# Accumulating half-size products in PSUM chains, gate rows on ScalarE, and a four-bank recurrence in a two-layer Hawk/HGRN2 step

## The chip, the cores and the metric

The kernel runs on one core of a Trainium2 chip. A core has TensorE (PE: matmuls, with its weight loads counted apart as PEld), VectorE (DVE), ScalarE (ACT), GpSimd (POOL) and SyncE (SP), each with its own instruction stream that is executed in order. The engines meet through semaphores. Matmuls write PSUM, which this kernel uses as eight banks of 128 x 512 fp32. The metric is the device time of one execution in microseconds, lower is better; a comparison uses the median of several runs.

## What is computed

Two layers over 1056 tokens (1024 of a prompt and 8 x 4 of decoding sequences), model width 1024, all in fp32. The first is an RG-LRU block. The second, the one that this change touches, is an HGRN2 block with 8 heads of width 128:

```python
u = (xn @ w_in).astype(jnp.float32)
q, f, iv, gate = jnp.split(u, 4, axis=-1)
q = jax.nn.silu(q).reshape(Bsz, T, H_B, DK_B)
log_g = jnp.logaddexp(jnp.log(lbh), jnp.log1p(-lbh) + jax.nn.log_sigmoid(f...))
k = -jnp.expm1(log_g)
v = iv.reshape(Bsz, T, H_B, DV_B)
o, S_T = _hgrn2_chunked(q, k, v, log_g, S0)
o = o * lax.rsqrt(jnp.mean(o * o, axis=-1, keepdims=True) + EPS) * o_gain...
y = (o.reshape(Bsz, T, INNER_B) * jax.nn.silu(gate)).astype(x.dtype)
return x + y @ w_out, S_T.astype(x.dtype)
```

So each head needs four projections of 128 rows (q, f, v and the output gate), then a gated linear recurrence, then a norm over the head. The gate g is `lbc + lc * tanh(f/2)` and the key is `lc - lc * tanh(f/2)`: two rows that are affine in one tanh.

## The kernel before

**fp32 from three passes.** Every fp32 product is split: weight and activation are each a high and a low part, and `mm3` (L240) issues three matmuls, high x high, high x low, low x high, that add up in PSUM. ACT makes the high part of a weight (L1425, `whi<-wraw`), POOL the low part (L322, `wlo<-wraw,whi`).

**Layer 1 by heads.** Heads 0 and 1 are projected in the plain way (`item`, L993, and `product`, 352 columns at a time). Heads 2 to 7 are projected by `seven` (L1398), two calls for each head: one with order `FQ` for the rows q and f (items 0 and 1), then one with order `GV` for the output gate and v (items 3 and 2). A call treats a pair of rows as a 2 x 2 block product (two halves of the 1024 inputs, two halves of the tokens) and computes it by seven products of half size in place of eight: product 1 to product 7, each 128 x 512 weights against 528 tokens. Each is done in two quarters x = 0 and 1 of 264 tokens, 12 matmuls each, into a fresh bank `ps`. In this text "6x0" is quarter 0 of product 6. With P1 to P7 for the products, the results are

- row a, first half: P1 + P2
- row a, second half: P1 + P6 + P5 + P3
- row b, first half: P1 + P6 + P7 + P4
- row b, second half: P1 + P6 + P7 + P5

Before, ACT copies P1 out of its bank (L1468), and every further sum is an addition by DVE, `plus` (L1496), that reads one bank and one SBUF tile of 264 columns: 14 in a call. The three `mm` banks rotate, so a product's quarter may start when the quarter three places earlier has been read.

`settle` (L1498) ends a row: tanh on ACT, then for q and the output gate a multiply on DVE (L1511), and for f two rows by POOL (L1505: the gate `Gs`, L1506: the key `b`), 264 columns at a time. `item` does the same for head 1 in chunks of 352 (L1009, L1011).

**The recurrence in four bursts.** It is computed by doubling levels 1, 2, 4, ..., 64. Each level scales half of two rows by products of gates (`scale`, L1022: DVE L1033 and a gate product L1042, ACT copies the other half, L1036) and PE multiplies small diagonal blocks (`diag`, L1047). DVE keeps the blocks of each level in `ad` with masked copies (`keep`, L1055), and four DVE copies put them on the diagonal of the attention tile `at` (L1114). The PE work of the recurrence is grouped into bursts that stand between products: burst 1 (levels 0 and 1; transposes of keys and values of the head before), burst 2 (levels 2 and 4; the states of the head before, which DVE chains in `SA`, L1232 and L1234), burst 3 (outputs of the head before, levels 8 and 16), burst 4 (its gating, levels 32 and 64). The letters b in an order string are the bursts: `FQ` = "12b675b43" holds bursts 3 and 4, `GV` = "126b754b3" bursts 1 and 2. The first call, for head 2, has `FQ0` = "126b74b35". Each burst takes five or four of the five `hg` banks in turn, one of them (`s`) for small matmuls of the decoding sequences.

**What sets the order.** All work of layer 1 is recorded with estimated costs in a `Flow` (L51); a list scheduler fixes each engine's order from priorities and due times, and the instructions are then emitted in that order. PE's work is recorded as `main`, so its order is the one of the code. What the other engines do in between is decided by the planner.

Of the kernel before, what the change touches and what calls it, by code (L numbers as in the profile page):

```python
# [19 lines left out]
ALU = mybir.AluOpType  # L20
# [6 lines left out]
NMM = 3  # L27
HC = 2
NM7 = 3
FQ0, FQ, GV = "126b74b35", "12b675b43", "126b754b3"  # L30
# [180 lines left out]
def tile_trunk(ctx: ExitStack, tc: tile.TileContext, xT, prm, hc, w0, wg, wo0, w1, wo1, s_in,  # L211
# [28 lines left out]
    def mm3(out, w, xh, xl, first, last):  # L240
        wh, wl = w
        T.matmul(out, wh, xh, start=first, stop=False)  # L242
        T.matmul(out, wh, xl, start=False, stop=False)  # L243
        T.matmul(out, wl, xh, start=False, stop=last)  # L244
# [681 lines left out]
    with ExitStack() as l1:  # L926
# [3 lines left out]
        mm, hg = cycle(banks8[:NMM]), cycle(banks8[NMM:])  # L930
# [62 lines left out]
        def item(h, i):  # L993


            def evac(c, ps, pk):
# [10 lines left out]
                if i == 1:  # L1007
                    g, (b, bk) = Gs, brow(h, 1)
                    pool(CH, lambda: G.tensor_scalar(g[:, q], t, lc[:, h:h + 1], lbc[:, h:h + 1], op0=ALU.mult, op1=ALU.add),  # L1009
                         (tk,), GK, 0)  # L1010
                    pool(CH, lambda: G.tensor_scalar(b[:, q], t, lcn[:, h:h + 1], lc[:, h:h + 1], op0=ALU.mult, op1=ALU.add),  # L1011
                         (tk,), bk, 0)
# [85 lines left out]
        def levels816(h, p8, pk):  # L1098
# [13 lines left out]
            for j in range(4):  # L1112
                w = slice(32 * j, 32 * j + 32)
                dve(256, lambda w=w: V.tensor_copy(at[w, :, w], ad[w]), (("ad",),), (("at", 0),), 3)  # L1114
# [6 lines left out]
        def levels3264(h, ps, pk):  # L1121
# [17 lines left out]
            p64, qk = next(hg)  # L1139
            pe(0.56, emit64, (*ak, *bk), (qk,))  # L1140
# [3 lines left out]
            for i in range(2):  # L1144
# [3 lines left out]
                moved(i, 256, odd[:64, i, :, 64:], p64[64 * i:64 * i + 64, :256].rearrange("p (u t) -> p u t", u=4), qk, ("at", 2, i))  # L1148
# [156 lines left out]
        def gated(h, s, sk):  # L1305
# [10 lines left out]
            o = s[:, 256:288]  # L1316
# [10 lines left out]
        def burst1(h):  # L1327
            s = next(hg)
            run(together([*([levels01(h, *s)] if h < H else []), *([keys_(h - 1, *s), values(h - 1, (1,), *s)] if h else [])]))

        def burst2(h):
            s = next(hg)
# [65 lines left out]
        def seven(h, a, b, order, at=()):  # L1398
# [44 lines left out]
            late, mid, low = places  # L1443
            places = low, mid, late
            for c in order:
# [9 lines left out]
                for x in range(2):  # L1455
                    ps, pk = next(mm)
                    ops = [operand(p, j, x) for j in range(4)]

                    def emit(ps=ps, ops=ops, hi=hi, lo=lo):
# [7 lines left out]
                    if p == 1:  # L1467
                        act(QT, lambda o=late[x][0], z=z[0]: S.copy(o, z), (pk,), (late[x][1],), 0)  # L1468
                    elif p == 2:
                        plus(mid[x], z, late[x])  # L1470
                        ending(a, first, *mid[x])
                    elif p == 6:
                        plus(late[x], z, late[x])
                    elif p == 7:
                        plus(low[x], z, late[x])
                    elif p == 3:
                        plus(late[x], z, late[x])
                    else:
                        t, o = second if p == 5 else first, mid[x] if next(q for q in steps if q in (4, 5)) == p else low[x]
                        if b == 2:  # L1480
                            plus((VT[:, t:t + QT], ("VT", t // QT)), z, low[x])
                            if t + QT == TOK:
                                thrice(vrep, VT[:, SEQ:], (("VT", 3),), "vrep")
                        else:
                            plus(o, z, low[x])
                            ending(b, t, *o)
                        if p == 5:
                            plus(late[x], z, late[x])
                    if p == [q for q in steps if q in (3, 5)][1]:
                        ending(a, second, *late[x])  # L1490
# [317 lines left out]
```

## Time and profile before

| | |
|---|---|
| time, median of 3 runs | 1086.44 us (1086.31 to 1087.67) |
| span of the profiled execution (its own time is not given; the span is 2.2 us under the median) | 1084.3 us |
| PE busy | 97% of the span |
| DVE busy | 82% |
| POOL busy | 56% |
| ACT busy | 51% |
| granted TensorE clock, mean | 0.993 |

The span falls into layer 0 (up to about 520 us), heads 0 and 1 of layer 1 (about 520 to 600 us), heads 2 to 7 in `seven` (about 600 to 960 us), and the output projection with the final norm. A row of the timeline gives start, duration, engine, line, operation, tiles and shape, and in brackets how long the engine had been idle before it and on whom it waited. A PE matmul of 264 columns is shown with about 0.28 us, but one starts every 0.12 us, since they overlap; PE counts as idle only when none is in flight.

### The profile page before, as it was taken

How to read it: one execution, taken by the hardware profiler on the slowest of the kernel's cores; microseconds unless marked ns; L12 is line 12 of the kernel's file. 1: busy time of each engine (PE TensorE's matmuls, PEld its weight loads, DVE VectorE, ACT ScalarE, POOL GpSimd, SP SyncE). 2: the span in 40 equal slices, each digit the busy share in tenths (PEclk: the TensorE clock that was granted, in tenths of full speed). 3: DMA queues.
4: the chain of work that ended last, by engine and by line, in shares of the span. 5: the costliest groups of instructions: out<-in, count | busy, mean ns of one | idle time of the engine just before them, and what ended most of it. 6: DMA issues, size and time to landing. Idle time of an engine off the chain costs nothing.

```text
span 1084.3 us, 25492 instructions
## 1 busy us (share of the span) xinstructions
PE 1056.6 (97%) x9972; PEld 1027.9 (95%) x9972; DVE 885.3 (82%) x1661; ACT 549.2 (51%) x1249; POOL 602.3 (56%) x600
## 2 busy tenths in 40 slices
PE   9999999999999999999999999999999999999997
PEld 9999999999999999999899899999998989899996
DVE  8999995897996886275989999989989898995436
ACT  6578657868666964143433444443343434452323
POOL 3425453363452537356665876858686776752545
PEclk9999999999999999999999999999999999999998
DMA  9211222124822776240210121212121212355204
GB/s 299 60 26 42 56 55 66 55 67 133 279 83 66 223 251 180 95 134 30 60 41 24 48 92 43 99 44 89 39 77 51 89 42 67 111 179 164 77 7 160
DMA packets 70119, 103.05 MB, mean 95 GB/s; under 512 B 9200, under 2 KB 51184, under 8 KB 70000
## 3 DMA queue, kind: packets, MB, share of 16 engines
q1 hardware_dynamic: 67696, 98.67, 29.5%
q10 hardware_dynamic: 2304, 2.77, 0.7%
q8 instruction: 78, 1.28, 0.5%
q14 instruction: 41, 0.34, 0.1%
HBM read 71.05 MB, written 25.49 MB: 89 GB/s over the span
## 4 chain that ended last, share of the span: by engine, by line
PE 75%; DVE 20%; issue 3%; DMA 1%; POOL 0%; ACT 0%; POOLq 0%; ACTq 0%; DVEq 0%; SPq 0%
PE mm L242 21%; PE mm L243 20%; PE mm L244 20%; DVE k L1496 3%; DVE R L1033 2%; DVE sg L1042 2%; DVE sg L1033 2%; DVE R L1511 1%; PE hg L566 1%; DVE tmp L1365 1%; PE hg L1214 1%; PE hg L242 1%; PE hg L243 1%; PE hg L244 1%; PE hg L1268 1%
## 5 line engine op out<-in xcount | busy, mean ns | idle before, releaser
L242 PE MATMUL mm<-xh,whi 128*128 128x352 f32 (+1 forms) x1143 | 360.6, 315 | 1.7 <-DVE k L1496 1.6
L243 PE MATMUL mm<-xl,whi 128*128 128x352 f32 (+1 forms) x1143 | 354.4, 310 | 0.9 <-DVE xl L322 0.9
L244 PE MATMUL mm<-xh,wlo 128*128 128x352 f32 (+1 forms) x1143 | 354.2, 310 | 0.0
L322 POOL TENSOR_TENSOR wlo<-wraw,whi 128x512 fp32r<-128x512 f32 (+2 forms) x132 | 181.9, 1385 | 145.2 <-ACT whi L377 84.2
L242 PEld LDWEIGHTS mm<-xh,whi 128*128 128x128 f32 x1143 | 215.9, 189 | 4.4 <-DVE k L1496 2.5
L243 PEld LDWEIGHTS mm<-xl,whi 128*128 128x128 f32 x1143 | 216.2, 189 | 2.6 <-DVE xl L322 1.1
L244 PEld LDWEIGHTS mm<-xh,wlo 128*128 128x128 f32 x1143 | 216.0, 189 | 0.0
L498 DVE SCALAR_TENSOR_TENSOR k<-xb,prm_sb,k 128x352 f32<-128x352 f32 (+2 forms) x144 | 90.1, 637 | 10.9 <-ACT k L495 6.2
L242 PE MATMUL mm<-t,whi 128*128 128x264 f32 (+1 forms) x306 | 89.9, 294 | 7.1 <-DVE k L1496 7.1
L243 PE MATMUL mm<-t,whi 128*128 128x264 f32 (+1 forms) x306 | 87.7, 286 | 0.0
L244 PE MATMUL mm<-t,wlo 128*128 128x264 f32 (+1 forms) x306 | 87.6, 286 | 0.0
L581 POOL TENSOR_TENSOR k<-X 128x352 f32<-128x352 f32 x36 | 43.9, 1227 | 47.4 <-DVE R L582 37.8
L242 PEld LDWEIGHTS mm<-t,whi 128*128 128x128 f32 x306 | 57.6, 188 | 8.6 <-DVE k L1496 7.9
L1496 DVE TENSOR_TENSOR k<-mm,k 128x264 f32<-128x264 f32 x144 | 60.0, 425 | 5.2 <-issue 1.3
L322 POOL TENSOR_TENSOR wlo<-R,whi 128x512 fp32r<-128x512 f32 x32 | 46.1, 1442 | 28.1 <-ACT whi L1425 26.8
L377 ACT CAST whi<-wraw 128x512 fp32r<-128x512 f32 (+2 forms) x83 | 46.0, 574 | 29.9 <-PE mm L243 18.2
L244 PEld LDWEIGHTS mm<-t,wlo 128*128 128x128 f32 x306 | 57.6, 188 | 0.0
L243 PEld LDWEIGHTS mm<-t,whi 128*128 128x128 f32 x306 | 57.6, 188 | 0.0
L1033 DVE TENSOR_TENSOR R<-R,sg 128x512 f32<-128x512 f32 (+1 forms) x48 | 52.6, 1096 | 0.2
L242 PE MATMUL mm<-yh,whi 128*128 128x352 f32 x153 | 49.9, 326 | 0.0
L244 PE MATMUL mm<-yh,wlo 128*128 128x352 f32 x153 | 49.4, 323 | 0.0
L243 PE MATMUL mm<-yl,whi 128*128 128x352 f32 x153 | 49.4, 323 | 0.0
(479 smaller groups left out, 2714.8 us busy)
## 6 DMA issues: line engine op xcount, KB each, us to landing
wraw<-in_w_dram SPq DMA_DIRECT2D x90, 256.0 KB, 2.8
wraw<-in_wo_dram SPq DMA_DIRECT2D x34, 192.0 KB, 2.5
si<-in_s_in_dram SPq DMA_DIRECT2D x8, 512.0 KB, 4.6
out_ss_out_dram<-si SPq DMA_DIRECT2D x8, 512.0 KB, 2.6
R<-in_w_dram SPq DMA_DIRECT2D x15, 256.0 KB, 2.6
sg<-x1b SPq DMA_DIRECT2D x21, 176.0 KB, 2.9
x<-sg SPq DMA_DIRECT2D x21, 176.0 KB, 2.0
R<-td SPq DMA_DIRECT2D x72, 44.0 KB, 2.0
```

Source lines behind the costliest of these rows:

```text
L242: T.matmul(out, wh, xh, start=first, stop=False)
L243: T.matmul(out, wh, xl, start=False, stop=False)
L244: T.matmul(out, wl, xh, start=False, stop=last)
L322: emit = lambda: e.tensor_tensor(b, x, a.bitcast(F32), op=ALU.subtract)
L377: act(m, lambda hi=hi, raw=raw, m=m: S.copy(hi[:, :m], raw[:, :m]), rk, (hk,), prio)
L498: dve(u, lambda src=src, dst=dst, sh=sh, k=k: V.scalar_tensor_tensor(dst, sh(src, k), pc("cw", 12 * k + m), dst, op0=ALU.mult, op1=ALU.add ...
L566: fl.add("PE", 0.62, lambda ps=ps, i=i, c=c: T.matmul(ps[:96, :CH], gs[:, i, :], ST[:96, chunk(c)], start=True, stop=True), (("gs",), *((" ...
L581: pool(CH, lambda x=x, a=a, b=b: G.tensor_tensor(x, a.bitcast(F32), b.bitcast(F32), op=ALU.add), (ak, bk), (xk,), 3)
L1033: dve(n // 2, lambda sv=sv, dv=dv, s=s, f=f: V.tensor_tensor(dv[:, :, s, :], sv[:, :, s, :], f, op=ALU.mult), (*sk, *gk), dk if i == o els ...
L1042: dve(nb, lambda: V.tensor_tensor(g2, gv[:, :, 0], gv[:, :, 1], op=ALU.mult), gk, (k2,), 3, True)
L1214: T.matmul(ps[:, n * 128:(n + 1) * 128], kt[:, 4 * i + n, :], vt[:, 4 * i + n, :], start=True, stop=True)
L1496: dve(QT, lambda: V.tensor_tensor(o[0], z[0], u[0], op=ALU.add), (z[1], u[1]), (o[1],), 0)
```

## The change

**Chains.** `mm` in `seven` no longer rotates over three banks. Four banks are split into two chains of two, one bank for each quarter: `chains[0]` takes products 1, 6, 7, 4, and `chains[1]` takes 2, 5, 3. Products 6, 7 and 4 do not start a new sum: their first matmul adds to what stands in the bank. ACT copies P1, P1+P6 and P1+P6+P7 out of the bank (L1481 in the new file), and after product 4 the bank holds the whole sum of row b's first half, which `settle` reads directly (for v, ACT copies it to `VT`, L1488). Product 3 adds to product 5's bank where 5 comes first, and `plus` (now L1504) is left with P2, P5 and P3: 6 in a call, 8 in the `FQ0` call, where 3 comes before 5. ACT copies 6 in a call in place of 2, and 2 more in a `GV` call.

**Order.** `GV` becomes "126b74b53": one product fewer stands between bursts 1 and 2, one more after burst 2.

**Gate rows.** The two affine rows of f go from POOL to ACT (`Identity` with a scale and a bias for each partition; L1513, L1514, and in `item`).

**Diagonal copies.** The four copies into `at` for each head go from DVE to ACT (L1112).

**Banks.** `hg` has four banks; levels 32 and 64 share one bank; `s` of bursts 1 and 2 comes from `side`, which is the fourth bank outside `seven` and the two banks of `chains[1]` inside it.

```diff
-FQ0, FQ, GV = "126b74b35", "12b675b43", "126b754b3"
+FQ0, FQ, GV = "126b74b35", "12b675b43", "126b74b53"
...
-        mm, hg = cycle(banks8[:NMM]), cycle(banks8[NMM:])
+        mm, side, hg = cycle(banks8[:NMM]), cycle(banks8[NMM:4]), cycle(banks8[4:])
+        chains = banks8[:2], banks8[2:4]
...
             for j in range(4):
                 w = slice(32 * j, 32 * j + 32)
-                dve(256, lambda w=w: V.tensor_copy(at[w, :, w], ad[w]), (("ad",),), (("at", 0),), 3)
+                act(256, lambda w=w: S.copy(at[w, :, w], ad[w]), (("ad",),), (("at", 0),), 3)
...
-            p64, qk = next(hg)
-            pe(0.56, emit64, (*ak, *bk), (qk,))
+            p64 = ps[:, 128:384]
+            pe(0.56, emit64, (*ak, *bk), (pk,))
...
         def burst1(h):
-            s = next(hg)
+            s = next(side)
...
                 for x in range(2):
-                    ps, pk = next(mm)
+                    ps, pk = chains[p in (2, 3, 5)][x]
+                    new = p in (1, 2, 5) or apart and p == 3
...
-                            mm3(ps[:, :QT], (hi[:, w], lo[:, w]), uh, ul, j == 0, j == 3)
+                            mm3(ps[:, :QT], (hi[:, w], lo[:, w]), uh, ul, new and j == 0, j == 3, True)
...
+                    if p in (1, 6, 7):
+                        o = {1: one, 6: two_, 7: three}[p][x]
+                        act(QT, lambda o=o[0], z=z[0]: S.copy(o, z), (pk,), (o[1],), 0)
                     elif p == 2:
-                        plus(mid[x], z, late[x])
-                        ending(a, first, *mid[x])
-                    elif p == 6:
-                        plus(late[x], z, late[x])
-                    elif p == 7:
-                        plus(low[x], z, late[x])
-                    elif p == 3:
-                        plus(late[x], z, late[x])
+                        plus(one[x], z, one[x])
+                        done(a, first, *one[x])
+                    elif p == 4:
+                        if b == 2:
+                            o = home(b, first, None)
+                            act(QT, lambda o=o[0], z=z[0]: S.copy(o, z), (pk,), (o[1],), 0)
+                        done(b, first, *z)
                     else:
...
                         if p == 5:
-                            plus(late[x], z, late[x])
+                            o = home(b, second, three[x])
+                            plus(o, z, three[x])
+                            done(b, second, *o)
+                        if p == 3 or apart:
+                            plus(two_[x], z, two_[x])
...
-                pool(QT, lambda: G.tensor_scalar(Gs[:, q], b, lc[:, h:h + 1], lbc[:, h:h + 1], op0=ALU.mult, op1=ALU.add), bk, (g,), 0)
-                pool(QT, lambda: G.tensor_scalar(b, b, lcn[:, h:h + 1], lc[:, h:h + 1], op0=ALU.mult, op1=ALU.add), bk, bk, 0)
+                act(QT, lambda: S.activation(Gs[:, q], b, AF.Identity, bias=lbc[:, h:h + 1], scale=lc[:, h:h + 1]), bk, (g,), 0)
+                act(QT, lambda: S.activation(b, b, AF.Identity, bias=lc[:, h:h + 1], scale=lcn[:, h:h + 1]), bk, bk, 0)
...
-        mm, hg = cycle(banks8[:NM7]), cycle(banks8[NM7:])
+        side = cycle(banks8[NMM - 1:4])
```

The planner makes a new order from this. Three places of a head in the middle of the run (heads 3 to 7 read alike) matter for the prediction. In these rows `hg` and `mm` are banks, `attnd` is `ad`, `attns` its small version for the decoding sequences, `R`, `a` and `sg` are the rows that the levels scale, `k` the homes of partial sums. The new file's lines stand 1 to 8 higher or lower than the old ones: L1033 is L1031, L1055 is L1053, L1496 is L1504, L1036 is L1034.

DVE from the scalings after burst 1 to the one that burst 2 waits for, before:

```order
L1033 TENSOR_TENSOR R<-R,ST 128x528
L1033 TENSOR_TENSOR a<-a,ST 128x528
L1496 TENSOR_TENSOR k<-mm,k 128x264
L1058 COPY_PREDICATED attns<-mask_86,hg 32x32
L1058 COPY_PREDICATED attns<-mask_87,hg 32x32
L1496 TENSOR_TENSOR k<-mm,k 128x264
L1176 TENSOR_TENSOR kst<-hg,kst 32x128
L1176 TENSOR_TENSOR vst<-hg,vst 32x128
L1033 TENSOR_TENSOR R<-R,sg 128x264x2
L1496 TENSOR_TENSOR sg<-mm,k 128x264
L1496 TENSOR_TENSOR k<-mm,k 128x264
L1033 TENSOR_TENSOR sg<-a,sg 128x264x2
```

and in the change:

```order
L1031 TENSOR_TENSOR R<-R,ST 128x528
L1031 TENSOR_TENSOR a<-a,ST 128x528
L1031 TENSOR_TENSOR R<-R,sg 128x264x2
L1031 TENSOR_TENSOR sg<-a,sg 128x264x2
L1174 TENSOR_TENSOR vst<-mm,vst 32x128
L1174 TENSOR_TENSOR kst<-mm,kst 32x128
L1056 COPY_PREDICATED attns<-mask_86,mm 32x32
L1056 COPY_PREDICATED attns<-mask_87,mm 32x32
```

The four scalings of levels 1 and 2 now follow each other at once; the additions and the small copies between them are gone or stand behind.

DVE from burst 2 to the additions of product 5, which the banks of product 3 wait for, in the change (before, these additions were of products three places away):

```order
L1053 COPY_PREDICATED attnd<-mask_88,hg 128x256
L1053 COPY_PREDICATED attnd<-mask_89,hg 128x256
L1031 TENSOR_TENSOR sg<-sg 128x128x4
L1230 COPY a<-hg 128x128
L1232 SCALAR_TENSOR_TENSOR a<-a,gp,hg 128x128 x3
L1056 COPY_PREDICATED attns<-mask_88,mm 32x32
L1232 SCALAR_TENSOR_TENSOR a<-a,gp,hg 128x128 x4
L1248 SCALAR_TENSOR_TENSOR si<-si,gp,hg 128x128
L1031 TENSOR_TENSOR R<-R,sg 128x128x4
L1504 TENSOR_TENSOR sg<-mm,k 128x264 x2
```

The whole chain of states and the scaling of level 4 stand ahead of the two additions.

ACT in the same call, from burst 1 to the copies of 7x0 and 7x1 (the two rows L1481), in the change:

```order
L1164 COPY kt<-hg 128x512 x2
L1164 COPY sg<-hg 128x512
L1034 COPY R<-R 128x264x2
L1172 CAST vst<-mm 96x128
L1172 CAST kst<-mm 96x128
L1481 COPY k<-mm 128x264
L1034 COPY sg<-a 128x264x2
L1176 COPY vts<-mm 32x128
L1481 COPY k<-mm 128x264
```

Each copy out of a chain's bank stands behind a copy (L1034) that waits for DVE's scaling of level 1.

More of the change, by code (lines that the diff above doesn't have):

```diff
@@ L1442, in seven, with done, home @@
                 split(p)
-            late, mid, low = places
-            places = low, mid, late
+            one, two_, three = places
+            apart = steps.index(3) < steps.index(5)
+            def done(i, t, c, ck):
+                if i == 2:
+                    if t + QT == TOK:
+                        thrice(vrep, VT[:, SEQ:], (("VT", 3),), "vrep")
+                else:
+                    ending(i, t, c, ck)
+            def home(i, t, o):
+                return (VT[:, t:t + QT], ("VT", t // QT)) if i == 2 else o
             for c in order:
@@ L1598, in tile_trunk @@
         splits(5, range(NCH), G)
-        mm, hg = cycle(banks8[:NMM]), cycle(banks8[NMM:])
+        side = cycle(banks8[NMM:4])
         raws = cycle([r for r in rawq if r[1][0] == "raw"])
```

37 lines of the change are left out of this document (12 added, 25 removed).

## The prediction

> **What bounds the kernel now.** I read the page first, then the busy time by stretches, then who PE waits for, and last the timeline around those waits. The page's first and fourth parts:
>
> ```profile
> span 1084.3 us, 25492 instructions
> PE 1056.6 (97%) x9972; PEld 1027.9 (95%) x9972; DVE 885.3 (82%) x1661; ACT 549.2 (51%) x1249; POOL 602.3 (56%) x600
> ...
> PE 75%; DVE 20%; issue 3%; DMA 1%; POOL 0%; ACT 0%; POOLq 0%; ACTq 0%; DVEq 0%; SPq 0%
> ```
>
> PE is the bound: 1084.3 - 1056.6 leaves it idle for 27.7 us, and no change that keeps its matmuls can win more. This one keeps them all: 7 products x 2 quarters x 12 matmuls in each of 12 calls. But 20% of the chain that ended last is DVE. By stretches (columns: length, then busy time and instructions of each engine):
>
> ```profile
> core 0: us, PE busy (x) PEld busy (x) DVE busy (x) ACT busy (x) POOL busy (x), PEclk, DMA share, GB/s
> ...
> 749.30:808.60 59.30, 57.42 (x809) 55.19 (x808) 53.66 (x102) 24.36 (x67) 41.80 (x38) 1.00 0.21 65
> ```
>
> That is one head of the middle run: PE idle for 1.9 us, DVE busy for 53.7 of 59.3. The granted clock is 1.00, so PE's rate is not in question. Who PE waits for, in heads 0 to 2 (520 to 630 us of the span; columns: total, times, longest) and behind them (630 to 990):
>
> ```profile
> PE hg L1051 <- DVE sg L1033: 2.3, 1, 2.3
> PE hg L1105 <- DVE a L1033: 1.6, 1, 1.6
> PE hg L1160 <- DVE si L1250: 1.4, 1, 1.4
> PE mm L243 <- DVE xl L322: 0.9, 1, 0.9
> PE hg L1136 <- DVE sg L1033: 0.5, 1, 0.5
> ...
> PE mm L242 <- DVE k L1496: 8.7, 9, 1.5
> PE hg L1051 <- DVE sg L1033: 3.0, 4, 0.8
> ```
>
> Every wait is for DVE, 18.4 us in all. The rest of the 27.7 us lies in the start and in the final norm, which the change leaves. Two kinds recur in each head:
>
> ```profile
> 755.87 1.26 DVE L1063 TENSOR_TENSOR R<-R,ST 128x1056 f32<-128x1056 f32 x1
> 757.04 0.42 DVE L1496 TENSOR_TENSOR k<-mm,k 128x264 f32<-128x264 f32 x1
> ...
> 757.52 0.39 PE L242 MATMUL mm<-t,whi 128*128 128x264 f32 x1 [1.15 <-DVE k L1496]
> ...
> 759.18 1.10 PE L1051 MATMUL hg<-R,a 128*32 128x64 f32 x64
> ...
> 762.02 0.37 PE L242 MATMUL mm<-t,whi 128*128 128x264 f32 x1
> ...
> 762.59 0.93 DVE L1055 COPY_PREDICATED attnd<-mask,hg 128x256 f32<-128x256 uint8 x2
> ...
> 764.48 0.70 DVE L1033 TENSOR_TENSOR a<-a,ST 128x528 f32<-128x528 f32 x1
> ...
> 769.06 3.25 DVE L1033 TENSOR_TENSOR sg<-a,sg 128x528 f32<-128x528 f32 x1
> ...
> 771.82 1.63 POOL L1433 TENSOR_TENSOR R<-R,wraw 128x512 f32<-128x512 f32 x1
> ...
> 772.46 0.75 PE L1051 MATMUL hg<-R,sg 128*32 128x32 f32 x64 [0.73 <-DVE sg L1033]
> ```
>
> At 757.5 a product waits until its bank is read: the addition is short (0.42), but stood behind the 1.26 us of L1063. Burst 1 starts at 759.18, has its first blocks ready 1.1 us later and lasts 2.8 us; DVE comes to its masked copies at 762.59, 2.3 us late. At 772.5 the second half of burst 2 waits for a scaling that took 3.25 us where the same shape took 0.70 at 764.48, while POOL worked beside it. So DVE is late, partly by its own load, partly stretched by POOL.
>
> [...]
>
> **The change part by part.**
>
> ```profile
> L1496 DVE TENSOR_TENSOR k<-mm,k 128x264 f32<-128x264 f32 x144 | 60.0, 425 | 5.2 <-issue 1.3 <-PE mm L244 1.2
> L1114 DVE COPY attn<-attnd 32x256 f32<-32x256 f32 x32 | 17.3, 541 | 0.5
> L1505 POOL TENSOR_SCALAR ST<-a,smalls 128x264 f32<-128x264 f32 x24 | 15.4, 647 | 4.0 <-ACT a L1504 4.0
> L1506 POOL TENSOR_SCALAR a<-a,smalls 128x264 f32<-128x264 f32 x24 | 19.6, 825 | 0.2
> L1468 ACT COPY k<-mm 128x264 f32<-128x264 f32 x24 | 8.6, 374 | 6.5 <-PE mm L244 5.9
> L495 ACT ACTIVATE k<-xb,prm_sb 128x352 f32<-128x352 f32 x24 | 16.4, 681 | 3.2 <-DVE sg L528 1.8 <-DVE xb L479 0.9
> ```
>
> *DVE load.* A head loses 28 - 12 = 16 additions of 0.425 (6.8 us) and four diagonal copies of 0.541 (2.2 us): DVE falls from 53.7 to about 44.7 us of 59.3. POOL loses 4 x (0.647 + 0.825) = 5.9 of its 41.8 us.
>
> *ACT load.* A head gains 8 copies for the chains and 2 for v at 0.374 (3.7 us), 8 gate rows and 4 diagonal copies. The trace of before has no ACT instruction of 264 columns with a scale and a bias; the nearest, L495 with 352 columns, takes 0.681, and the plain copy of 264 takes 0.374, so a gate row lies between the two and I take 0.6, nearer to L495 since it is the same operation (8 x 0.6 = 4.8). A diagonal copy has 32 x 256 elements; I take 0.374 for it too (1.5). ACT rises from 24.4 to about 34.4 us of 59.3: room enough on average, and free where it does not queue.
>
> *What goes.* In `seven` I count the two recurring waits, 8.7 + 3.0 = 11.7 us, as gone, since DVE has 9 us less to do in each head and the additions that the first kind waited for (products 1, 6, 7 and 4) are now copies by an engine that is 58% busy. At the end of head 1, burst 4 waits 0.5 and 1.4 us for DVE, which ahead of it has additions of head 2's products 2, 6, 7 and 4 in its order (8 x 0.425 = 3.4 us); those of product 2 alone stay, 2.6 us go, so I count the 1.9 us as gone too. The waits of 2.3 and 1.6 us in heads 0 and 1 stay: DVE's order ahead of them is the same list of `build` additions, and no addition of `seven` lies there. The 0.9 us stays: product 5 of head 2 still waits for its operand, made by the same DVE and ACT steps. Gone: 11.7 + 1.9 = 13.6 us.
>
> *What comes.* A product that adds to its bank must wait until the bank has been read. Where a chain's products follow each other, only one quarter lies between, and the trace shows how long that is:
>
> ```profile
> 780.63 0.38 ACT L1468 COPY k<-mm 128x264 f32<-128x264 f32 x1
> ...
> 782.10 0.38 ACT L1468 COPY k<-mm 128x264 f32<-128x264 f32 x1 [1.09 <-PE mm L244]
> ```
>
> The two quarters of a product are 1.47 us apart, and the copy starts with the end of the product's last matmul, about 0.16 us behind the next one's first issue (0.28 against 0.12). The copy needs 0.38, so 1.47 - 0.16 - 0.38 leaves 0.9 us. Before, two quarters lay between, and 2.4 us were left. The places are 6 to 7 in `FQ` and 7 to 4 in `GV` (ACT), and 5 to 3 in `GV` (DVE).
>
> For the ACT places I add nothing. In `GV` 7x0's copy stands behind the ACT copy of level 1's scaled row; counted from burst 1's start, that scaling can end about 2.7 us in (blocks at 1.1, two masked copies 0.9, scaling 0.70), the ACT copy 0.7 us later, and 7x0 ends at 4.5 us. That ACT works off its queue in time is the cover; if it is gone, the cost is that of the last rival.
>
> For 5 to 3 the order rows give a wait. Burst 2 before, with the first product behind it:
>
> ```profile
> 770.95 0.73 PE L1051 MATMUL hg<-R,a 128*32 128x32 f32 x62
> ...
> 773.60 0.91 DVE L1055 COPY_PREDICATED attnd<-mask,hg 128x256 f32<-128x256 uint8 x2
> 774.40 0.98 DVE L1033 TENSOR_TENSOR sg<-sg 128x512 f32<-128x512 f32 x1
> ...
> 775.62 1.11 DVE L1234 SCALAR_TENSOR_TENSOR a<-a,gp,hg 128x128 f32<-128x128 f32 x3
> ...
> 776.04 0.29 PE L242 MATMUL mm<-xh,whi 128*128 128x264 f32 x1
> ...
> 778.70 0.68 DVE L1033 TENSOR_TENSOR R<-R,sg 128x512 f32<-128x512 f32 x1
> ```
>
> Without its 0.73 us wait the burst lasts 776.04 - 770.95 - 0.73 = 4.4 us, and 3x0 wants to start 2 x 1.47 later, at 7.3. DVE can start the masked copies when both levels are multiplied, at 1.5; they take 0.8, the scaling 0.9, the eight states 8 x 0.37 = 3.0, the small masked copy 0.1, one update of `si` (the size of a state) 0.4, the second scaling 0.7 to 1.1, and 5x0's addition 0.42. That is 7.7 to 8.1, and 3x0 waits 0.4 to 0.8 us. If DVE comes to burst 2 as late as before (773.60, 2.65 us in), it is 1.9; if the states overlap better, nothing. I take 0.8, since L1033 seldom runs at its shortest. Heads 3 to 7 have this order, so 5 x 0.8 = 4.0 us; in head 2 the additions stand earlier.
>
> **Sum.** -13.6 + 4.0 = -9.6 us: the span falls from 1084.3 to 1074.7, and the median, 2.1 us above it, from 1086.4 to 1076.8.
>
> **The rivals.** *All waits of `seven` go*, the one at product 3 too: 13.6 us, 1072.8. For it: DVE has 14 us of slack per head. Against: the order rows put all of burst 2's work on DVE ahead of the addition.
>
> *The wait at burst 2 grows.* With `GV`'s new order only products 7 and 4 lie between bursts 1 and 2, four quarters instead of six, 2.9 us less. Before, the last scaling (769.06 + 3.25) ended 13.1 us behind burst 1's start; the new order wants it at 9.4 (2.8 for the burst, 5.9 for the quarters, 0.7 for level 2). DVE sheds four additions inside (1.7 us) and, I expect, the 2.3 us by which it came late; that brings it to 9.1. If half of its lateness stays and POOL stretches the scalings as before, about 1 us of wait is left, if all stays 2.0. At 1.4 us in six heads it takes back 8.4: 1085.2, no change. Against it: the scalings now follow each other at once, and unstretched they need 2.8 us.
>
> *The copies out of the banks come late* (slower than before). In-order ACT holds a chain's copy behind an instruction that waits for DVE or POOL, and PE, which had 2.4 us of tolerance, has 0.9. If the copy is as late as DVE's additions were at their worst (1.5 us of wait beyond 2.4, so 3.9 us late), each place costs 3 us a head. From 1.6 us a head on (9.6 / 6) the change loses; with one such place, six heads cost 18: 1076.8 + 18 = 1095, and at half that lateness 1083. Against: ACT copied P1 within 0.1 us of its end in the rows above.
>
> [...]
>
> **How the numbers follow.** My forecast (1074.5 to 1081) has a chance of 0.50, all waits gone 0.15, the grown wait at burst 2 (1081 to 1088) 0.20, late copies (above 1086) 0.15. A measurement of this kernel can tell about 0.2%, 2.2 us, from no change. Of the third case a bit over half is still faster than 1084.3: faster 0.50 + 0.15 + 0.12 = 0.77; same 0.08 from it; slower 0.15. The range holds 8 in 10 from 1072 to 1086; the forecast's own is 1074.5 to 1081.
>
> **What would show it.** Right: about 74 additions instead of 168; DVE near 45 us and ACT near 34 in a head; a head of about 58.0 us instead of 59.3 (59.3 - 2.1 + 0.8); PE's waits for L1504 only ahead of product 3. Wrong: PE waiting for ACT copies (L1481) ahead of product 7 or 4, or for L1031 in burst 2 by more than 0.7 us; then the third or fourth case has come. If the waits of heads 0 and 1 move by more than a microsecond, my reading of the planner's order there was wrong.

## The result, and the profile after

| | before | after |
|---|---|---|
| median | 1086.88 us (4 runs, 1086.31 to 1087.67) | 1077.35 us (4 runs, 1075.47 to 1077.86) |
| ratio, 95% interval | | 0.991 (0.9896 to 0.9924) |
| span of the profiled execution | 1084.3 us | 1073.7 us |

1076.8 was forecast, in a range of 1072 to 1086. The number held, and the change is faster by 9.5 us, four times what such a measurement can tell. The forecast's reasons held less well than its number. First the page after, its first and fourth parts:

```profile
span 1073.7 us, 25345 instructions
PE 1053.0 (98%) x9972; PEld 1024.5 (95%) x9972; DVE 808.2 (75%) x1535; ACT 611.1 (57%) x1395; POOL 558.0 (52%) x546
...
PE 82%; DVE 14%; issue 1%; DMA 1%; ACT 1%; POOL 0%; SPq 0%; POOLq 0%; ACTq 0%; DVEq 0%
```

PE is idle for 20.7 us in place of 27.7, and DVE's part of the chain that ended last falls from 20% to 14%. The kernel after, busy time in a stretch of about one head (columns as in the prediction):

```profile
750.00:809.00 59.00, 58.23 (x817) 56.15 (x816) 41.58 (x83) 34.45 (x91) 37.35 (x30) 1.00 0.20 70
```

This stretch is 1.2 us longer than a head. Cut at burst 1 (752.00 to 809.80), ACT is busy for 33.8 us, near the forecast 34.4, and DVE for 40.3, which is 4.4 below the forecast 44.7. The prices of the moved work were right: the kernel after, groups by shape, of ACT:

```profile
L1481 ACT COPY k<-mm 128x264 f32<-128x264 f32 x72 | 27.3, 379 | 28.2 <-PE mm L243 28.1
...
L1513 ACT ACTIVATE ST<-a,smalls 128x264 f32<-128x264 f32 x24 | 14.6, 607 | 0.6
...
L1112 ACT COPY attn<-attnd 32x256 f32<-32x256 f32 x32 | 12.9, 404 | 3.0 <-DVE rst L1292 2.6
```

A gate row takes 0.61 us (0.6 was taken), a diagonal copy 0.40 (0.374), a chain copy 0.38. Who PE waits for from 520 to 990 us, the kernel after (total, times, longest):

```profile
PE mm L241 <- DVE sg L1504: 4.5, 7, 0.8
PE mm L241 <- DVE attns L1056: 2.7, 1, 2.7
PE hg L1049 <- DVE R L1061: 2.0, 1, 2.0
PE mm L241 <- ACT xh L1590: 1.4, 1, 1.4
PE mm L242 <- DVE xl L321: 0.8, 1, 0.8
```

11.6 us with one of 0.2 that is left out, in place of 18.4. The old recurring waits are gone, and the new one stands where the forecast put it, ahead of product 3:

```profile
768.51 0.76 DVE L1504 TENSOR_TENSOR sg<-mm,k 128x264 f32<-128x264 f32 x2
768.99 0.39 PE L241 MATMUL mm<-xh,whi 128*128 128x264 f32 x1 [0.77 <-DVE sg L1504]
```

To see where the time went, the start of burst 1 in heads 1, 3 and 6 is a good marker. The timeline of before, then of after:

```profile
570.90 0.81 PE L1051 MATMUL hg<-R,a 128*32 128x64 f32 x43
...
700.01 0.49 PE L1051 MATMUL hg<-R,a 128*32 128x64 f32 x20
...
877.71 0.49 PE L1051 MATMUL hg<-R,a 128*32 128x64 f32 x20
```

```profile
567.59 0.60 PE L1049 MATMUL hg<-R,a 128*32 128x64 f32 x28 [2.02 <-DVE R L1061]
...
694.31 0.88 PE L1049 MATMUL hg<-R,a 128*32 128x64 f32 x48
...
867.59 0.60 PE L1049 MATMUL hg<-R,a 128*32 128x64 f32 x28
```

| stretch | change, by the markers | the forecast's terms in it |
|---|---|---|
| up to head 1's burst 1 | -3.3 | 0 (the waits of 2.3 and 1.6 us were to stay) |
| to head 3's burst 1 | -2.4 | -3.7 (1.9 of burst 4, 1.8 of the additions) |
| to head 6's burst 1 (three heads) | -4.4 | -3.7 (6.1 gone, 3 x 0.8 come) |
| to the end of the span | -0.5 | -2.1 (3.7 gone, 2 x 0.8 come) |
| sum | -10.6 | -9.5 |

A head of the middle run takes 57.8 us after 59.2; 58.0 was forecast. Two of the four stretches are off by 1.3 to 1.6 us and one by 3.3, in both directions.

### The profile page after: what moved, and what is told of

The parts are those of the page before. It is cut to its first block, busy times and chain, and to the rows that moved or that the text cites. A ratio compares the mean times of both kernels' runs of the same rounds, so it can differ in the third digit from the quotient of the medians.

```text
span 1073.7 us, 25345 instructions
## 1 busy us (share of the span) xinstructions
PE 1053.0 (98%) x9972; PEld 1024.5 (95%) x9972; DVE 808.2 (75%) x1535; ACT 611.1 (57%) x1395; POOL 558.0 (52%) x546
## 4 chain that ended last, share of the span: by engine, by line
PE 82%; DVE 14%; issue 1%; DMA 1%; ACT 1%; POOL 0%; SPq 0%; POOLq 0%; ACTq 0%; DVEq 0%
PE mm L241 23%; PE mm L242 22%; PE mm L243 22%; PE hg L1049 2%; DVE R L1363 1%; DVE R L1031 1%; PE hg L1266 1%; PE hg L565 1%; DVE tmp L1363 1%; PE hg L1158 1%; DVE a L1232 1%; PE hg L1268 1%; DVE sg L1031 1%; PE hg L241 1%; PE hg L242 1%
## 5 line engine op out<-in xcount | busy, mean ns | idle before, releaser
L321 POOL TENSOR_TENSOR wlo<-wraw,whi 128x512 fp32r<-128x512 f32 (+2 forms) x131 | 175.9, 1351 | 168.7 <-ACT whi L376 83.6
L580 POOL TENSOR_TENSOR k<-X 128x352 f32<-128x352 f32 x36 | 44.9, 1256 | 47.8 <-DVE R L581 38.6
L321 POOL TENSOR_TENSOR wlo<-R,whi 128x512 fp32r<-128x512 f32 x33 | 49.9, 1511 | 32.8 <-ACT whi L1423 28.9
L1504 DVE TENSOR_TENSOR k<-mm,k 128x264 f32<-128x264 f32 x62 | 26.5, 430 | 41.5 <-PE mm L243 41.4
L1031 DVE TENSOR_TENSOR R<-R,sg 128x512 f32<-128x512 f32 (+1 forms) x48 | 50.4, 1050 | 0.1
```

What stands on the lines that cost most here:

```text
L321: emit = lambda: e.tensor_tensor(b, x, a.bitcast(F32), op=ALU.subtract)
L580: pool(CH, lambda x=x, a=a, b=b: G.tensor_tensor(x, a.bitcast(F32), b.bitcast(F32), op=ALU.add), (ak, bk), (xk,), 3)
L1031: dve(n // 2, lambda sv=sv, dv=dv, s=s, f=f: V.tensor_tensor(dv[:, :, s, :], sv[:, :, s, :], f, op=ALU.mult), (*sk, *gk), dk if i == o els ...
L1504: dve(QT, lambda: V.tensor_tensor(o[0], z[0], u[0], op=ALU.add), (z[1], u[1]), (o[1],), 0)
```

## The experiments

Theories. The one on record: DVE is late by its load of additions and diagonal copies; chains take the additions away; the price is the wait ahead of product 3. Rival: POOL's instructions stretch DVE's two-input ones, and the gate rows' move from POOL is what helped. A third came up on the way: the place of DVE's instructions against POOL's decides, and any edit that makes the planner draw another order moves it. Ratios are to the kernel before on the same chip, with 95% intervals.

### One part of the change undone

**gates_pool**: the changed kernel with

```diff
-  act(QT, lambda: S.activation(Gs[:, q], b, AF.Identity, bias=lbc..., scale=lc...), bk, (g,), 0)
-  act(QT, lambda: S.activation(b, b, AF.Identity, bias=lc..., scale=lcn...), bk, bk, 0)
+  pool(QT, lambda: G.tensor_scalar(Gs[:, q], b, lc..., lbc..., op0=ALU.mult, op1=ALU.add), bk, (g,), 0)
+  pool(QT, lambda: G.tensor_scalar(b, b, lcn..., lc..., op0=ALU.mult, op1=ALU.add), bk, bk, 0)
```

and the same two rows in `item`.

> The changed kernel with the gate rows back on POOL (in item and in settle); everything else of the change is kept. My theory: the gain comes from additions that no longer stand in DVE's order ahead of PE, so the rows' engine hardly matters in heads 3 to 7: POOL gets about 5.9 us a head back, ACT loses about 5, PE still waits 0.8 us for L1504 ahead of product 3 and for little else; 1076.5 to 1079.5 us. In heads 0 and 1, where the change left DVE's order alone, the waits of 2.3 and 1.6 us come back if it was the rows that moved POOL there (+2). Rival, relief from POOL: the scalings were short because POOL has less to do beside them; then scalings stretch again, burst 2 waits for L1031 in most heads (0.7 us x 6 or more), and the time is 1081 to 1086.

Measured: 1083.38 us, 0.9963 (0.9950 to 0.9975). By the time, the rival was right; by the trace, neither. Who PE waits for, 520 to 990 us:

```profile
PE mm L241 <- DVE attns L1058: 3.2, 2, 2.4
...
PE hg L1051 <- DVE sg L1033: 2.0, 1, 2.0
PE mm L241 <- DVE sg L1506: 1.9, 5, 0.4
PE mm L242 <- DVE xl L321: 1.6, 1, 1.6
PE hg L1105 <- DVE a L1033: 1.4, 1, 1.4
```

The rival asks for waits for scalings (L1033) in burst 2 of most heads; PE waits for them in head 0 alone. From head 3 on a head takes 57.8 to 58.4 us, nearly as after. The loss lies ahead of it: the waits that the prediction puts in heads 0 and 1 are back (2.0 and 1.4 us, both in head 0), new ones of 1.6 and 1.0 us stand around 627 us, and the clock was lower at both places:

```profile
540.00:550.00 10.00, 6.80 (x149) 6.66 (x150) 9.10 (x16) 3.15 (x6) 3.48 (x3) 0.66 0.18 57
```

A granted clock of 0.66 over 10 us is some 6.8 us at half speed (in the kernel before it was 0.50 from 544.5 to 547.0 us). Where PE waits anyway it costs nothing, so the loss is less than the 3.4 us that this would make. Over 625 to 635 us the clock is 0.66 again.

### The moves to ACT alone, together and apart

**act_only, gates_only, diag_only**: the kernel before with the gate rows on ACT (the diff above, read upwards) and with

```diff
-  dve(256, lambda w=w: V.tensor_copy(at[w, :, w], ad[w]), (("ad",),), (("at", 0),), 3)
+  act(256, lambda w=w: S.copy(at[w, :, w], ad[w]), (("ad",),), (("at", 0),), 3)
```

both in act_only, one each in the other two.

> The kernel before with only the gate rows and the diagonal copies on ACT; no chains, the old banks and the old order. My theory: the 28 additions a head stay in DVE's order, so most of the 8.7 us of waits for the addition (L1496 of before) stays; DVE loses 2.2 us a head, and the waits for scalings (3.0 us behind 630 us) may shrink: 1083 to 1086.5 us. Rival, relief from POOL: these two moves alone bring most of the gain; 1077 to 1081, with DVE's scalings near 0.7 us.

> The kernel before with only the gate rows on ACT; the diagonal copies stay on DVE, no chains, old order. Theory now: DVE was late because POOL's instructions stretched its own, so 5.9 us less of POOL in a head takes about as much off DVE (53.6 to 47 or 48), and the waits of 2.1 us a head go without a single addition removed: a head of 57 to 57.5 us, 1076 to 1079. Rival, the 2.2 us of diagonal copies did it in act_only: a head of 58.5 or more, 1082 to 1086.

> The kernel before with only the diagonal copies on ACT. Theory now (stretch by POOL): DVE loses its 2.2 us and no more (about 51.4 a head), POOL runs as before, most of the waits stay: a head of 58.5 to 59.2 us, 1083 to 1087. Rival (the copies did it): a head near 57, 1076 to 1079.

Measured: act_only 1075.35 us, 0.9880 (0.9863 to 0.9897); gates_only 1085.45, 0.9982 (0.9972 to 0.9991); diag_only 1085.32, 0.9982 (0.9972 to 0.9992). act_only came out below both of its ranges, gates_only in its rival's and diag_only in its theory's. Without one addition removed, the two moves together win 1.2%, no less than the whole change; each alone 0.2%. So the additions need not go for the waits to go, against the theory on record, and the parts don't add up, against the rival too. Busy times from one burst 1 to the next, gates_only, diag_only and act_only:

```profile
755.97:815.13 59.16, 57.55 (x807) 55.08 (x806) 48.80 (x101) 28.34 (x75) 36.56 (x30) 1.00 0.19 65
```

```profile
757.35:815.78 58.43, 57.30 (x806) 55.02 (x805) 47.84 (x96) 26.26 (x71) 43.71 (x38) 1.00 0.20 66
```

```profile
754.95:811.88 56.93, 56.93 (x807) 54.92 (x806) 45.60 (x97) 30.13 (x79) 38.32 (x29) 1.00 0.20 68
```

In gates_only DVE is 4.8 us a head less busy than before (53.6), and the head is as long as before. In diag_only it is 5.8 us less busy, and a product still waits 1.1 us in each head. What differs between gates_only and act_only is when DVE comes to burst 1. Timeline of gates_only (burst 1 starts at 755.97) and of act_only (754.95):

```profile
759.35 0.93 DVE L1053 COPY_PREDICATED attnd<-mask,hg 128x256 f32<-128x256 uint8 x2
...
765.31 2.33 DVE L1031 TENSOR_TENSOR sg<-a,sg 128x528 f32<-128x528 f32 x1
...
768.38 0.39 PE L242 MATMUL mm<-t,whi 128*128 128x264 f32 x1 [1.13 <-DVE k L1494]
```

```profile
756.12 0.95 DVE L1053 COPY_PREDICATED attnd<-mask,hg 128x256 f32<-128x256 uint8 x2 [0.50 <-PE hg L1049]
...
762.18 2.34 DVE L1031 TENSOR_TENSOR sg<-a,sg 128x528 f32<-128x528 f32 x1
```

In gates_only DVE starts the masked copies 3.4 us behind the start of the burst, as before; in act_only 1.2 us, and there DVE waits for PE. The same stretched scaling (2.33 and 2.34 us) then makes a product wait in the one and not in the other. Why one move alone does not bring DVE there in time stays open.

### The chains alone, and the banks alone

**chains_old**: gv_old (below) with gate rows and diagonal copies where they were. **banks_only**: the kernel before with only

```diff
-        mm, hg = cycle(banks8[:NMM]), cycle(banks8[NMM:])
+        mm, side, hg = cycle(banks8[:NMM]), cycle(banks8[NMM:4]), cycle(banks8[4:])
...
-            p64, qk = next(hg)
-            pe(0.56, emit64, (*ak, *bk), (qk,))
+            p64 = ps[:, 128:384]
+            pe(0.56, emit64, (*ak, *bk), (pk,))
...
         def burst1(h):
-            s = next(hg)
+            s = next(side)
```

and the same in burst 2 and behind `seven`.

> The chains alone, with the four-bank recurrence: the changed kernel with GV in its old order, gate rows on POOL, diagonal copies on DVE. The theory on record (additions) expects nearly all of gv_old's gain: 1068 to 1072. Stretch by POOL expects heads 3 to 7 somewhat above 57 us, since the chains alone free 6 us of DVE, but heads 0 to 2 as in gates_pool, with the waits of 2.0 and 1.4 us in head 0 and those around 627 and 659 us, and the lower granted clock behind them: 1075 to 1081.

> The kernel before with only the four-bank recurrence: hg has four banks, the fourth bank of the other set serves the small matmuls of bursts 1 and 2, levels 32 and 64 share a bank. In seven its products keep their three rotating banks. Theory: no burst is waiting for a bank in the trace of before (every wait there is for operands or for the additions), so nothing is gained or lost: 1085.5 to 1088.5 us. Rival: with one bank less a burst waits for its readers on DVE, a few tenths in each head: 1089 to 1093.

Measured: chains_old 1072.54 us, 0.9861 (0.9846 to 0.9876), between the two expectations. Its additions are gone, and yet PE waits 1.4, 1.1 and 0.9 us in heads 3, 4 and 6, ahead of product 5, whose bank burst 1's small matmuls have used. In head 6 the profile names DVE's last copy out of that bank (`vst`, L1176); in the other two it names ACT, but that copy ends 0.14 to 0.15 us ahead there too.

banks_only 1077.01, 0.9912 (0.9890 to 0.9933), against both. This edit moves no work between engines and takes none away, and yet no wait is left in heads 3 to 6. The changed kernel holds this edit too. A head of banks_only, cut at burst 1:

```profile
754.71:811.44 56.73, 56.73 (x806) 54.84 (x806) 46.71 (x101) 24.86 (x67) 44.07 (x38) 1.00 0.20 67
```

PE never idles there, and DVE, with 101 instructions as before, is busy for 46.7 us (48.3 in the head ahead of it) where it was 53.6. That is about as much as in diag_only (47.8), where a product waits in each head, so it is not the load that tells the two apart. The groups of three heads show which instructions grew shorter, before and then banks_only:

```profile
L1496 DVE TENSOR_TENSOR k<-mm,k 128x264 f32<-128x264 f32 x72 | 30.3, 427 | 3.3 <-issue 1.0 <-PE mm L244 0.7
L1511 DVE SCALAR_TENSOR_TENSOR R<-R,k 128x264 f32<-128x264 f32 x12 | 13.6, 1130 | 0.0
L1033 DVE TENSOR_TENSOR sg<-a,sg 128x528 f32<-128x528 f32 x3 | 9.7, 3248 | 0.0
```

```profile
L1496 DVE TENSOR_TENSOR k<-mm,k 128x264 f32<-128x264 f32 x72 | 30.2, 426 | 7.6 <-PE mm L244 6.3
L1511 DVE SCALAR_TENSOR_TENSOR R<-R,k 128x264 f32<-128x264 f32 x12 | 7.7, 640 | 0.0
L1033 DVE TENSOR_TENSOR sg<-a,sg 128x528 f32<-128x528 f32 x3 | 2.2, 746 | 0.0
```

The additions, which read one tile from PSUM and one from SBUF, keep their 0.43 us; these two groups with two SBUF inputs go from 1.13 to 0.64 and from 3.25 to 0.75. Over the three heads, summed by what they read, DVE's instructions with an input from PSUM take 73.2 us before and 73.4 in banks_only, those with two SBUF inputs 94.3 and 75.6 (some of them longer: `a<-a,ST` goes from 0.70 to 1.43), and the copies of L1114, with one SBUF input, 7.3 and 6.1. In a head DVE's order differs by a handful of places (two multiplies of `settle` behind a scaling instead of ahead, a gate product and a small masked copy moved by a few rows). Which of these swaps decides was not tried, nor whether it is the order or the new use of the banks itself that matters.

In heads 3 to 6, DVE starts its masked copies 3.4 us behind the start of burst 1 before and in gates_only, 2.4 to 2.5 in diag_only and chains_old, 1.5 to 1.9 in banks_only, and 1.2 to 1.3 in act_only, gv_old (below) and the changed kernel. In the first four PE then waits in each head (but for one of chains_old), in the others no such wait recurs; what is left in the changed kernel is its own wait at product 3. gates_pool does not fit so well: DVE starts 2.6 us behind, and PE waits 0.4 us at product 3 and once 0.75 elsewhere. No run moved this start alone, so it goes with the waits and is not shown to cause them.

### The order of GV, and the wait at product 3

**gv_old**: the changed kernel with

```diff
-FQ0, FQ, GV = "126b74b35", "12b675b43", "126b74b53"
+FQ0, FQ, GV = "126b74b35", "12b675b43", "126b754b3"
...
-            apart = steps.index(3) < steps.index(5)
+            apart = steps.index(3) < steps.index(5) or b == 2
```

**p5_copy**: the changed kernel with

```diff
-                            plus(o, z, three[x])
+                            if b == 2:
+                                act(QT, lambda o=o[0], z=z[0]: S.copy(o, z), (pk,), (o[1],), 0)
+                                plus(o, o, three[x])
+                            else:
+                                plus(o, z, three[x])
```

**act_order**: act_only with `GV` = "126b74b53".

> The changed kernel with GV in its old order, 126b754b3: product 3 comes behind burst 2 and starts a fresh sum (it can't add to product 5's bank, which burst 2 uses between), so DVE makes two more additions in each GV call. My theory: the waits of 0.77 us ahead of product 3 (four heads, 3.1 us, and 0.3 in head 7) go, nothing takes their place since six quarters stand between the bursts again, and head 2's 2.7 us stays, since the bank of burst 2 is needed 1.5 us behind it in either order: 1073 to 1075 us. Rival, the load of DVE counts and not its order: 0.85 us more on DVE in a head costs up to as much on PE: 1077 to 1082.

> The changed kernel, its order kept; in GV ACT copies product 5 out of its bank (into v's rows) and DVE adds the stored sum in place afterwards, so product 3 waits for ACT and not for DVE. My theory: ACT is free there, the bank is read 0.5 us behind product 5's end, and the waits of 0.77 us (four heads) and 0.25 go; head 2's 2.7 us stays, its 0.34 and 0.84 go: 1072.5 to 1075 us. Rival: the DVE addition now reads two SBUF tiles and is stretched beside POOL, or ACT's copy stands behind a copy that waits for DVE; then the wait only changes its name and the time stays at 1077 to 1080.

> act_only (before with gate rows and diagonal copies on ACT) and GV in the new order 126b74b53; no chains, so products 5 and 3 use different banks. If the new order costs by itself, because DVE has four quarters instead of six between the bursts, DVE is late at burst 2 or at the products behind it: 1078 to 1084. Rival, it costs only through the chain (product 3 waits for the reading of product 5's bank): 1075 to 1077, no wait that act_only has not.

Measured: gv_old 1067.42 us, 0.9807 (0.9787 to 0.9826); p5_copy 1072.73, 0.9862 (0.9840 to 0.9883); act_order 1078.14, 0.9921 (0.9905 to 0.9937). p5_copy came in as expected: no wait at product 3 is left, its heads take 56.7 us in place of 57.8, and head 2's wait stays, at 3.2. act_order has no recurring wait in heads 3 to 6 either: its heads take 57.0 us, as in act_only (56.9), so in the middle run the order costs only through the chain. Elsewhere it is slower: its time lies in the theory's range, 2.8 us above act_only's, and the intervals lie apart. Its burst 2 waits for a scaling in head 2 (1.1 us, 0.7 in act_only) and in head 7 (1.0, where act_only waits 1.2 for an addition), and 2.4 and 0.5 us come at the start of the output projection. gv_old gained far more than the 3 us expected. Who PE waits for, 520 to 990 us (one of 0.3 us left out), and a head:

```profile
PE hg L1049 <- DVE R L1061: 2.0, 1, 2.0
PE mm L1083 <- DVE k L1504: 1.6, 1, 1.6
PE mm L241 <- ACT sg L1034: 1.3, 1, 1.3
```

```profile
692.13:748.91 56.78, 56.78 (x807) 54.90 (x806) 40.26 (x82) 33.72 (x89) 36.56 (x29) 1.00 0.21 68
```

The wait at product 3 and what hangs on it are worth 1.0 us a head (57.8 to 56.8), 5 us in five heads. Head 2's waits are 2.9 us in place of 3.9, and those at the start of the output projection (1.4 and 0.8) are gone. That makes some 8 of the 10.1 us between the two profiled spans (1073.7 and 1063.6); the rest was not followed up. The changed kernel's granted clock is 1.00 in every 10 us up to 1060 us, and gv_old's mean over its profiled execution is 0.999. The 1.3 us in head 2 stand ahead of product 5, as the waits of chains_old do. gv_old beats both kernels, and the intervals of its ratio and of the changed kernel's (0.9903 to 0.9939, below) lie apart.

### Two tries to take gv_old's largest wait away

**gv_spot7**: gv_old with `SPOTS` = (7, 9, 0, 2) in place of (6, 9, 0, 2). In this kernel head 0's values of the last chunk are read after head 1's v stands there, so its outputs are not the reference's. **gv_add**: gv_old with the planner's cost of `build`'s sums raised, `dve(1.6 * n, ...)` for `dve(n, ...)` in `add`.

> gv_old with head 1's burst 1 one product later (SPOTS begins with 7 in place of 6), since PE waits 2.0 us there for the gate product L1061, which waits for the last gate row on ACT. Theory: a product of 3.8 us covers that wait: 1065 to 1066 us, burst 1 of head 1 without a wait. Rival: burst 1 and burst 2 of head 1 then stand only two products apart, and burst 2 waits for DVE's scalings by as much or more: 1067 to 1069.

> gv_old, and the planner counts the sums and differences of build 1.6 times as long (its numbers alone change, no instruction is added or taken away). In gv_old ACT stood 1.4 us at a cast of build, behind DVE, with the tanh of head 1's last gate chunk queued behind it, and PE then waited 2.0 us for own_gate. Theory: the planner puts that tanh ahead of the cast, and the 2.0 us go: 1064 to 1066 us. Rival: all orders behind it are drawn anew, and another pair of DVE and POOL instructions meets in the wrong order; waits of 1 to 3 us elsewhere in heads 0 to 2: 1067 to 1071.

Measured: gv_spot7 1072.53 us, 0.9859 (0.9844 to 0.9873); gv_add 1070.59, 0.9850 (0.9831 to 0.9869). The 2.0 us went in both, and both are slower than gv_old. gv_spot7 has the waits of 1.7 and 2.2 us of head 0 back. In gv_add one wait of 4.3 us stands at the first addition of head 2:

```profile
PE mm L241 <- DVE k L1504: 4.3, 1, 4.3
```

gv_add missed as its rival said. gv_spot7 is slower than both of its ranges: the rival looked for a wait at burst 2 of head 1, and what came are waits in head 0 and one of 1.7 us at head 2's first addition. In both, an order drawn anew moved the waits of heads 0 to 2 elsewhere.

### The changed kernel once more

**after_again** has no edit.

> The changed kernel, unchanged, with the others of this call. If the stretches of lower granted clock behind PE's waits are chance, this profile may show one or two (1.7 us each) where the first showed none ahead of the final norm, with the same waits: 1075 to 1078.5 us. If they follow from the kernel, the profile shows none again, and all PE waits are within 0.2 us of the first's.

Measured: 1078.01 us, 0.9921 (0.9903 to 0.9939); its profiled execution spans 1077.6 us, 3.9 more than the first. The waits are the same up to the output projection (2.0 at head 1's burst 1, 2.7 in head 2, 0.8 ahead of product 3 from head 3 on), except that the 0.3 and 0.8 us behind head 2's 2.7 are missing; at the projection 3.0 stand for the 1.4 and 0.8 of the first. The clock is not. The stretch behind head 2's wait, the first execution and then the second:

```profile
650.00:660.00 10.00, 8.58 (x66) 8.16 (x67) 9.32 (x25) 4.28 (x10) 2.59 (x2) 1.00 0.12 40
```

```profile
650.00:660.00 10.00, 8.02 (x50) 7.59 (x51) 9.47 (x25) 3.47 (x7) 2.75 (x3) 0.83 0.11 33
```

0.17 of 10 us is 1.7 us; the second pays it here, behind head 1's 2.0 us and behind the 3.0 us, the first nowhere ahead of the final norm. The same kernel, with the same waits ahead of it, pays it in one execution and not in the other.

## Why the prediction was right, and where it was not

**Right: the two terms of the recurring part.** The 8.7 and 3.0 us that were counted as gone have left the list of waits. For 3x0 0.8 us was taken: it waits 0.77 to 0.80 in heads 3 to 6; in head 7, which was counted too, it is 0.25. By the markers a head of the middle run gained 1.5 us where 1.3 was forecast. The adding-up of DVE's work ahead of 3x0 is slightly off: its terms make 7.8 to 8.2 us, not 7.7 to 8.1, which leaves 0.5 to 0.9 for the wait. The waits were counted at their length, and they cost somewhat more: a head without waits takes 56.7 us (banks_only, p5_copy), 2.5 less than before, where the waits add up to 2.1. Nor is PE's busy time fixed by its matmuls, as "no change that keeps its matmuls can win more" takes it to be: the same 9972 are busy for 1056.6 us before and 1053.0 after, and the 806 of a head for 57.1 us before and 56.8 in gv_old. The load of ACT and the prices of its new instructions were right, and the 0.9 us of tolerance was enough: no product waits for a chain copy (L1481), and burst 2 waits for no scaling (L1031), so the third and fourth cases did not come.

**Wrong: the cause of the first term.** The prediction counts the waits as gone "since DVE has 9 us less to do in each head", and its sum takes nothing for the stretch by POOL. act_only keeps every addition and loses the waits; banks_only keeps all work where it was and loses them too; gates_only takes 4.8 us off DVE and keeps them. DVE's load does not tell them apart: 47.8 us a head in diag_only, which keeps waits of 1.1 us, and 46.7 to 48.3 in banks_only, which has none. So the step that failed is the one from DVE's load to its lateness. The stretching that the prediction read off its 3.25 us row and then left out of the sum was the other half: the shortening of instructions with two SBUF inputs is worth 6 us a head in banks_only, nearly as much as the 6.8 us of additions. DVE's forecast load was probably too high for the same reason. The chains are one of several edits after which DVE comes to burst 1 in time; that they do it more surely than another order is not shown, and what brings DVE there in time stays open.

**Wrong: "The waits of 2.3 and 1.6 us in heads 0 and 1 stay".** The prediction named a move of more than a microsecond as the sign that its reading there is wrong. They went (both were in head 0), 2.0 us came at head 1's burst 1, and the clock stayed up. Of the four scalings of levels 4 and 8 in head 0, the first two before, and then the first and the last after:

```profile
538.06 3.16 POOL L322 TENSOR_TENSOR wlo<-wraw,whi 128x512 fp32r<-128x512 f32 x2
538.32 1.77 DVE L1033 TENSOR_TENSOR R<-R,sg 128x512 f32<-128x512 f32 x1
540.01 1.75 DVE L1033 TENSOR_TENSOR sg<-sg 128x512 f32<-128x512 f32 x1
```

```profile
537.38 3.27 POOL L321 TENSOR_TENSOR t<-R,t 128x264 fp32r<-128x264 f32 x1 [2.31 <-ACT t L1366]
537.55 0.68 DVE L1031 TENSOR_TENSOR R<-R,sg 128x512 f32<-128x512 f32 x1
...
539.36 0.67 DVE L1031 TENSOR_TENSOR a<-sg 128x512 f32<-128x512 f32 x1
```

Same work; before, POOL works beside them and the four take 1.77, 1.75, 1.24 and 1.22 us, and after, all four run at 0.67 or 0.68 while one POOL instruction, which took 0.79 in the kernel before (at 537.32 us), is drawn out to 3.27. In both kernels one of the two engines is drawn out, DVE in the first and POOL in the second; by what means, the rows do not show.

**Wrong: "in head 2 the additions stand earlier", so that nothing comes there.** 3.9 us came. The second quarter of product 5 waits until DVE has read burst 2's bank:

```profile
642.15 4.46 DVE L1519 SCALAR_TENSOR_TENSOR sg<-sg,k 128x264 f32<-128x264 f32 x1
642.56 1.27 POOL L321 TENSOR_TENSOR wlo<-wraw,whi 128x512 fp32r<-128x512 f32 x1
643.79 1.30 POOL L321 TENSOR_TENSOR wlo<-R,whi 128x512 fp32r<-128x512 f32 x1
645.05 1.27 POOL L1431 TENSOR_TENSOR wraw<-R,wraw 128x512 f32<-128x512 f32 x1
...
650.24 0.39 PE L241 MATMUL mm<-xh,whi 128*128 128x264 f32 x1 [2.70 <-DVE attns L1056]
```

A multiply that takes 0.42 us in most heads took 4.46 beside three POOL instructions in a row, and the masked copy that frees the bank stood behind it.

**Wrong by omission: the clock.** "PE's rate is not in question" was read from one head. In the kernel before, the clock was 0.83 of full over 540 to 550 and over 620 to 630 us, 3.4 us in all, which the first profile after did not pay. Together with the 0.9 us ahead of product 5 of head 2, which the forecast kept and which went too, this made about 5 us by the markers of the 1.9 forecast for burst 4 of head 1, and head 2's new waits took half of it back.

So the number was right in part by luck, because errors met: heads 0 and 1 gave 3.3 us that were not forecast, head 2 and the output projection took back 3.9 and 2.1, and the recurring part held.

## What to carry to other kernels

Compare each instruction's duration with the shortest of its shape before you count an engine's load: here the time by which DVE's instructions grew shorter in banks_only (6 us a head) was nearly as large as the additions that the change removed (6.8), and no work was moved for it. Where a planner draws the order, add a control edit that moves no work (as banks_only) before you credit a part of a change; 9.7 us came from one. When two products add up in one bank, and the second waits until the first sum is read, give the second a fresh bank and a place further behind (gv_old), or let an engine that is free copy the first sum out (p5_copy): either was worth 1.0 us a head here.

## What the runs showed of the hardware

**A wait can cost more than its length.** After waits of 1.4 to 4.3 us, often but not always, the granted clock fell to a half for some 3.4 us, which costs up to 1.7 us of PE's time. In windows of half a microsecond, the kernel before has 0.51 over 544.0 to 544.5 us, 0.50 up to 547.0 and 0.58 over the next, which makes 3.4 us at half, behind waits of 2.3 and 1.6 us that ended at 541.8 and 544.2; and 0.51 over 622.5 to 623.0, 0.50 up to 625.5 and 0.57 over the next, behind waits of 0.5 and 1.4 us that ended at 620.1 and 622.2. In gv_add the clock was 0.82 and 0.84 over the two halves of 620 to 630 us, with the wait of 4.3 us that ended at 623.1. In gates_pool and act_order it was 0.66 over 540 to 550 us, which makes twice that. Waits of 2.0 and 2.7 us paid it in one execution of the changed kernel (0.83 over 565 to 575 and over 650 to 660 us) and not in another (1.00 over both). Why some waits are followed by it and others are not, no run shows. Whether this is why a kernel's runs spread over 2 to 3 us is open: the mean clock of after_again's runs does not follow their times (1077.18 us at 0.993, 1078.57 at 0.996).

**An instruction of either engine was drawn out over several of the other's in a row.** In the changed kernel one of DVE lasted through three of POOL's (4.46 us for 0.42), and one of POOL through four of DVE's (3.27 us for 0.8).
